# Expert stage rebuilt: weights split in 1024-column pieces, half of down taken whole, result rows without the residual

## The chip, the core and the metric

The kernel runs on one core of a Trainium2 chip. The metric is device time in microseconds for one launch. Before the change three runs took 1353.7, 1354.76 and 1357.26 us (median 1354.76). The profiled execution, from which every row below comes, took 1354.12 us, of which the profile's span holds 1352.3.

## The reference, cut to what matters

Two decoder layers over 1040 tokens (16 learned ones and 1024 of the input) of 1024 channels, float32. Layer 0 mixes by causal pooling, layer 1 by latent attention with 8 heads. Each layer ends with the same mixture of experts, and this is what the change is about:

```
p_g = softmax(x @ wr_g + br_g);  g = argmax(p_g)              # one of 4 groups
logit = x @ wr_e + br_e;  top 2 of the 8 experts of group g
gate = p_g[g] * softmax(the two logits)
for each of the two:  y = (silu(x @ w_gate[e]) * (x @ w_up[e])) @ w_down[e]
h = h + sum of gate * y over the two                          # 1024 -> 256 -> 1024 per expert
```

The output is the normed `h` of the last 1024 tokens. All 32 experts of a layer are evaluated: 32 x 3 MB of weights per layer are read from DRAM.

## The kernel before

The program has four stages: layer 0's mixer and router (to about 107 us), layer 0's experts (to about 437), latents, attention and layer 1's router (to about 977), layer 1's experts and the final norm.

**Products.** TensorE takes a float32 product in one of two ways. *Whole*: the float32 operands as they are. *In parts*: each operand is split into a rounded high part (a ScalarE copy to float32r, L1224) and a low remainder (a VectorE subtraction, L1225), and three products high x high, high x low, low x high are added up (`mm3`, L1229 to L1231).

**The expert loop** (`Moe.run`, L872) goes over e = 0 to 32 and works in one round on expert e's gate and up products and on expert e-1's down product. A gather (L776) brings up to 96 token rows of `h_d` from DRAM into a buffer `xg`. TensorE transposes them (`xpose`, L794), VectorE multiplies by the norm's gain (L796, two times 384 columns). Of the eight 128-row steps of gate and of up, four run whole (`whole`, L817) and four in parts (`halves`), on weights split in pieces of 512 columns (`piece`, four buffers). Silu and product give `hm` (L841, L842), two transposes and a split give `hT` (`turn`, L851), and `down` runs twelve passes of 512 columns into `py`, all in parts. `rows` (L870, VectorE) computes `py * gate + xg` in place in `xg`; a scatter (L782) writes the 96 rows to `y_d`, where each token has one row for its first expert and one for its second. The scatters of a layer are declared independent of each other, since their rows differ.

**The residual** is carried by the rows: the mixer and the attention's output are scaled (`PART`), so that `h_d` holds a quarter or a half of `h`, the gates are scaled alike, and the two rows of a token add up to the whole `h`. The next stage (`Mid.ask`, `add`) and the end (`final`) therefore read two tensors of 128 tokens each and add them.

**Order of the work.** Each engine runs its instructions in the order in which the program issues them. Around the experts that order is written by hand in `Moe.run`; in the other stages a planner (`Sched`) orders tasks by costs and due times that stand in the code. A ring of 17 slots of 1 MB holds the weights: SyncE issues the next load when a slot comes free. GpSimd issues gathers (four experts ahead, nine `xg` buffers) and scatters on one queue, in program order. Weights of the first 17 slots are loaded while the router still works.

The lines that the prediction speaks of, as they stand before:

```python
self.k.nc.vector.scalar_tensor_tensor(y[:CAP, c], py[:CAP], wt, y[:CAP, c], op0=OP.mult, op1=OP.add)   # rows, L870
for o in self.scat:
    k.tc.declare_no_dep(st.ins, o.ins, reason="rows of other slots")                                  # scatter in run
nc.sync.dma_start(out=self.h_d[t * 128:t * 128 + n, :], in_=k.h[t][:n])                               # store_tasks, L410
s.op("V", ready, 1130, lambda: add(h, h, c, op=OP.add), lambda end: then(i, c, end))                  # Mid.add2, L1660
c = [[m.fetch(t, j) for j in range(2)] for t in range(NT)]                                            # final
```

## Time and profile before

| | |
|---|---|
| median of three runs | 1354.76 us |
| profiled execution, its span | 1354.12 us, 1352.3 us |
| TensorE busy | 1257.1 us, 93% of the span |
| VectorE busy | 1063.2 us, 79% |
| ScalarE busy | 751.3 us, 56% |
| GpSimd busy | 306.7 us, 23% |
| DMA moved | 284.96 MB, mean 211 GB/s |

How to read it: PE is TensorE's matmul, PEld its weight loads (which overlap), DVE VectorE, ACT ScalarE, POOL GpSimd, SP SyncE; a q behind the name is the engine's sequencer, which issues DMAs. "L1224" is a line of the kernel. Ends of matmuls are modelled, so the distance from one start to the next says how long one takes, not the duration. In brackets stands how long the engine was idle before an instruction and what ended that. Times are in us, in groups also ns for the mean of one. A row by stretch gives its length, then the busy time and number of instructions of PE, PEld, DVE, ACT and POOL in this order, the granted clock, the DMA engines' busy share and GB/s. A row of a timeline gives start, duration, engine, line, operation, out<-in, shapes and number; a row of a DMA view gives number, size and the us from issue to landing. The granted clock (PEclk) is 1.00 at 2.4 GHz and 0.50 at 1.2 GHz.

### The profile page before, as it was taken

What the parts mean: (1) busy time and instruction counts of PE and PEld (TensorE: products, weight loads), DVE (VectorE), ACT (ScalarE), POOL (GpSimd) and SP (SyncE); (2) the same over time, 40 slices, a digit from 0 to 9 for tenths busy, and PEclk for the clock granted to TensorE, in tenths of its full rate; (3) what the DMA queues carried; (4) which work ended last, traced back from release to release, by engine and by line L of the source; (5) the groups of instructions that cost most, each with busy time, mean ns of one, the idle gap of its engine ahead of it and who ended that gap; (6) DMA issues with size and microseconds to landing.
All of it is one profiled execution on the core that took longest, in us unless ns stands there. A gap on an engine that the chain in (4) does not pass through costs nothing. (4 is left out here: it accounts for less than half of the span.)

```text
span 1352.3 us, 22774 instructions
## 1 busy us (share of the span) xinstructions
PE 1257.1 (93%) x8027; PEld 1091.9 (81%) x8027; DVE 1063.2 (79%) x2591; ACT 751.3 (56%) x1597; POOL 306.7 (23%) x443
## 2 busy tenths in 40 slices
PE   7988999999998899999999999999699999999950
PEld 5977888888886799898998998989588888888830
DVE  5777888888888886767778766678878888888857
ACT  3436655555565654656565556555466555556532
POOL 0113121121111352022231232221312112112013
PEclk8998999999999899999999999999699999999975
DMA  8936999999980800100000010048699999999236
GB/s 300 409 127 207 363 364 361 350 368 361 361 283 26 267 25 1 57 24 28 21 25 25 5 32 16 17 161 283 248 319 368 364 350 361 357 346 349 88 137 276
DMA packets 78763, 284.96 MB, mean 211 GB/s; under 512 B 20017, under 2 KB 27441, under 8 KB 62258
## 3 DMA queue, kind: packets, MB, share of 16 engines
q1 hardware_dynamic: 64306, 249.60, 50.8%
q0 software_dynamic: 14336, 33.84, 7.5%
q8 instruction: 65, 1.06, 0.3%
q14 instruction: 56, 0.46, 0.1%
HBM read 262.09 MB, written 37.81 MB: 222 GB/s over the span
## 5 line engine op out<-in xcount | busy, mean ns | idle before, releaser
L1229 PE MATMUL gu<-wp,xT 128*96 128x256 f32 x512 | 147.3, 288 | 0.0
L1231 PE MATMUL gu<-wp,xT 128*96 128x256 f32 x512 | 143.4, 280 | 0.0
L1230 PE MATMUL gu<-wp,xT 128*96 128x256 f32 x512 | 143.3, 280 | 0.0
L782 POOL DMA_INDIRECT y_d<-xg,di x46 | 45.5, 989 | 360.4 <-DVE xg L870 348.4
L1225 DVE TENSOR_TENSOR wp<-slotB,wp 128x512 fp32r<-128x512 f32 x160 | 106.9, 690 | 22.7 <-ACT wp L1224 21.8
L1229 PE MATMUL py<-wp,hT 128*96 128x512 f32 x256 | 113.1, 442 | 0.8 <-ACT hT L1224 0.8
L1224 ACT ACTIVATE wp<-slotB 128x512 fp32r<-128x512 f32 x160 | 96.0, 626 | 23.4 <-PE py L1231 19.7
L1231 PE MATMUL py<-wp,hT 128*96 128x512 f32 x256 | 101.8, 398 | 0.2
L1230 PE MATMUL py<-wp,hT 128*96 128x512 f32 x256 | 101.0, 394 | 0.0
L2121 POOL TENSOR_TENSOR hh<-hh,wt 128x512 f32<-128x512 f32 x56 | 72.4, 1292 | 111.3 <-ACT wt L2120 110.6
L1224 ACT ACTIVATE xT<-xq 128x384 fp32r<-128x384 f32 x64 | 33.6, 526 | 109.5 <-DVE xq L796 109.5
L1229 PEld LDWEIGHTS gu<-wp,xT 128*96 128x96 f32 x512 | 84.8, 166 | 0.1
L1231 PEld LDWEIGHTS gu<-wp,xT 128*96 128x96 f32 x512 | 83.2, 162 | 0.0
L1230 PEld LDWEIGHTS gu<-wp,xT 128*96 128x96 f32 x512 | 82.9, 162 | 0.1
L817 PE MATMUL gu<-slotB,xq 128*96 128x256 f32 x320 | 75.6, 379 | 0.0
L1957 ACT ACTIVATE P<-bank,sm 128x400 f32<-128x400 f32 (+3 forms) x112 | 59.5, 539 | 25.7 <-DVE sm L1947 25.5
L1710 DVE TENSOR_TENSOR T<-bank,T 128x512 fp32r<-128x512 f32 (+2 forms) x112 | 53.6, 495 | 20.8 <-ACT T L1706 19.9
L796 DVE TENSOR_TENSOR xq<-pt,ffg 128x384 f32<-128x384 f32 x128 | 64.9, 548 | 4.5 <-PE pt L794 4.5
L2124 DVE SCALAR_TENSOR_TENSOR hh<-bank,ri,hh 128x512 f32<-128x512 f32 x72 | 53.5, 746 | 17.0 <-PE bank L1231 16.6
L870 DVE SCALAR_TENSOR_TENSOR xg<-py,table,xg 96x512 f32<-96x512 f32 x92 | 64.4, 738 | 3.0 <-PE py L1231 2.9
L1225 DVE TENSOR_TENSOR wp<-hh,wp 128x512 fp32r<-128x512 f32 x82 | 54.8, 690 | 11.3 <-ACT wp L1224 10.9
L841 ACT ACTIVATE hm<-gu,table 96x256 f32<-96x256 f32 x64 | 30.0, 469 | 58.4 <-PE gu L1231 58.4
(375 smaller groups left out, 3891.7 us busy)
## 6 DMA issues: line engine op xcount, KB each, us to landing
slotB<-w_up SPq DMA_DIRECT2D x20, 1024.0 KB, 11.2
slotB<-w_down SPq DMA_DIRECT2D x20, 1024.0 KB, 13.7
slotB<-w_gate SPq DMA_DIRECT2D x20, 1024.0 KB, 14.6
hh<-w_gate SPq DMA_DIRECT2D x11, 1024.0 KB, 12.6
hh<-w_up SPq DMA_DIRECT2D x10, 1024.0 KB, 8.3
hh<-w_down SPq DMA_DIRECT2D x10, 1024.0 KB, 9.0
slotR<-w_gate SPq DMA_DIRECT2D x10, 1024.0 KB, 13.4
slotR<-w_up SPq DMA_DIRECT2D x10, 1024.0 KB, 10.7
```

The lines of the kernel that those rows point to most:

```text
L796: nc.vector.tensor_tensor(x[q], pt, self.r.g[:, 4 * q:4 * q + 4].unsqueeze(2).to_broadcast([128, 4, CAP]), op=OP.mult)
L817: nc.tensor.matmul(gu[:CAP, f * FE:f * FE + FE], lhsT=x[0][:, j], rhs=w[:, j], start=(f == 0 and j == 0), stop=False)
L870: self.k.nc.vector.scalar_tensor_tensor(y[:CAP, c], py[:CAP], wt, y[:CAP, c], op0=OP.mult, op1=OP.add)
L1224: nc.scalar.activation(dH, src, AF.Copy)
L1225: nc.vector.tensor_tensor(dL, src, dH.bitcast(F32), op=OP.subtract)
L1229: nc.tensor.matmul(out, lhsT=aH, rhs=bH, start=start, stop=False)
L1230: nc.tensor.matmul(out, lhsT=aH, rhs=bL, start=False, stop=False)
L1231: nc.tensor.matmul(out, lhsT=aL, rhs=bH, start=False, stop=stop)
L1710: nc.vector.tensor_tensor(dL, src, dH.bitcast(F32), op=OP.subtract)
L1957: nc.scalar.activation(self.P[hd, qp][a][:, x0:x0 + xe], tt[:, :xe], AF.Exp, bias=sm[:, 3:4], scale=SCALE, accum_out=sm[:, x:x + 1])
L2121: done(end), s.op("G", end + s.LAT, 1170, lambda: nc.gpsimd.tensor_tensor(k.h[i][:, cs], k.h[i][:, cs], x, op=OP.add), lambda end: s.relea ...
L2124: s.op("V", now + s.LAT, 70 + 1.04 * 512, lambda: nc.vector.scalar_tensor_tensor(k.h[i][:, cs], p, self.ri[hd, i], k.h[i][:, cs], op0=OP.m ...
```

## The change

- **Pieces.** Weights are split 1024 columns at a time (`piece(e, f, q)`: matrix f, half q), with three buffers instead of four. Gate and up run wholly in parts (48 passes of 256 columns). Of down's two 128-row steps the first runs whole, the second in parts.
- **Order in a round.** The first halves of expert e+1's gate and up (`G`, `U`) are split in round e, behind down; `G1`, `wd` and `U1` in their own round. x of expert e+1 is transposed, scaled (one instruction of 768 columns) and split early in round e. Expert 0 runs its first halves whole.
- **Rows.** `rows` is one ScalarE instruction of 1024 columns, `py * gate`, without the residual; `PART` is gone.
- **Layer 0's rows**: the next stage reads `h_d` and both rows and adds three tensors; two buffers are taken for each tile; the first two tiles of `h_d` are read at the end of the expert stage (`Mid.ahead`).
- **Layer 1's rows**: `h` is stored to `h_d` and to `y_d`, and each scatter adds its rows to `y_d` in DRAM. Entries without a token go to 96 rows behind the tokens'. The scatters are no longer declared independent. `final` reads one tensor.
- Six `xg` buffers, gathers three ahead. `final` takes the tiles in other groups; the constant `tri` is loaded with a later part.

```diff
-WHOLE = 4
-NX = 9
-GA = 4
+NX = 6
+GA = 3
...
+        self.sum = layer == 1
+        self.y_d = k.tc.dram_tile([S + CAP if self.sum else 2 * L, D], F32, name=f"y_d{layer}")
...
+    def targets(self, di, row, off):
+        V = self.k.nc.vector
+        if self.sum:
+            V.tensor_scalar(di, row, self.junk_row[:CAP], None, op0=OP.min)
+        else:
+            V.tensor_tensor(di, row, off, op=OP.add)
...
+            if self.sum:
+                late.append(t)
+                while late and (t not in self.tiles[-2:] or t == self.tiles[-1]):
+                    x = late.pop(0)
+                    nc.sync.dma_start(out=self.y_d[x * 128:x * 128 + 128, :], in_=k.h[x])
...
+        if self.r.sum:
+            return nc.gpsimd.indirect_dma_start(
+                out=self.r.y_d, out_offset=bass.IndirectOffsetOnAxis(ap=didx, axis=0),
+                in_=y[:CAP], in_offset=None, bounds_check=S + CAP - 1, oob_is_err=True, compute_op=OP.add)
...
+    def xpose(self, xg, fine=False):
+        pt = self.psum.tile([128, 2, 512], F32, name="pt", tag="pt", bufs=1)[:, :, :4 * CAP]
+        x = k.mws.tile([128, 8, CAP], F32, name="xq", tag="xq", bufs=1)
+                nc.tensor.transpose(pt[:, q, j * CAP:(j + 1) * CAP], xv[:CAP, 4 * q + j], k.ident[:CAP, :CAP])
+        n = 2 if fine else 1
+        w = 2 // n
+        for i in range(n):
+            a, b = i * w, (i + 1) * w
+            nc.vector.tensor_tensor(x[:, 4 * a:4 * b].rearrange("p (a b) c -> p a b c", a=w),
+                                    pt[:, a:b].rearrange("p a (b c) -> p a b c", b=4),
+                                    self.r.g[:, 4 * a:4 * b].rearrange("p (a b) -> p a b", a=w).unsqueeze(3).to_broadcast(
+                                        [128, w, 4, CAP]), op=OP.mult)
+    def part(self, x, a=0):
+        xs = [self.k.mws.tile([128, 8, CAP], F32R, name=f"xT{i}", tag=f"xT{i}", bufs=2) for i in range(2)]
+        split(self.k, xs[0][:, a:], xs[1][:, a:], x[:, a:])
+        return xs
+    def piece(self, e, f, q):
+        src = self.w(e, f)
+        src = src[:, q] if f == 2 else src[:, 4 * q:4 * q + 4]
+        t = [k.mw.tile([128, 1024], F32R, name=f"wp{i}", tag=f"wp{i}", bufs=PIECES) for i in range(2)]
+        if f < 2:
+            t = [x.rearrange("p (a b) -> p a b", a=4) for x in t]
+        split(k, *t, src)
+    def up(self, gu, xs, wp, f, q):
+        for j in range(4):
+            mm3(self.k.nc, gu[:CAP, f * FE:f * FE + FE], xs[0][:, 4 * q + j], xs[1][:, 4 * q + j], wp[0][:, j], wp[1][:, j],
+                q == 0 and f == 0 and j == 0, q == 1 and f == 1 and j == 3)
+    def whole(self, gu, x, e, f):
+        w = self.w(e, f)
+        for j in range(4):
+            self.k.nc.tensor.matmul(gu[:CAP, f * FE:f * FE + FE], lhsT=x[:, j], rhs=w[:, j], start=(f == 0 and j == 0), stop=False)
...
+    def turned(self, ph):
+        h0 = k.mws.tile([128, CAP], F32, name="hT", tag="hT", bufs=1)
+        hs = [k.mws.tile([128, CAP], F32R, name=f"hT{i}", tag=f"hT{i}", bufs=1) for i in range(2)]
+        nc.scalar.activation(h0, ph[:, 0], AF.Copy)
+        split(k, hs[0], hs[1], ph[:, 1])
+        return h0, hs
+    def down(self, e, h, wp):
+        nc, w = self.k.nc, self.w(e, 2)
+        py = self.psum.tile([128, 2, 512], F32, name="py", tag="py", bufs=1)
+        cs = [slice(q * 512, q * 512 + 512) for q in range(2)]
+            nc.tensor.matmul(py[:CAP, q], lhsT=h[0], rhs=w[:, 0, cs[q]], start=True, stop=False)
+        for q in range(2):
+            mm3(nc, py[:CAP, q], *h[1], wp[0][:, cs[q]], wp[1][:, cs[q]], False, True)
+        return py
+    def rows(self, py, wt, y):
+        self.k.nc.scalar.activation(y[:CAP], py[:CAP].rearrange("p a b -> p (a b)"), AF.Copy, scale=wt)
...
-            for o in self.scat:
+            for o in () if r.sum else self.scat:
                 k.tc.declare_no_dep(st.ins, o.ins, reason="rows of other slots")
             self.scat.append(st)
...
-        x = self.xpose(xgs[0])
-        wp = self.up_pieces(0)
-        x = self.part(x)
-        hm = None
+        x = self.xpose(xgs[0], fine=True)
+        xs, G, U, hm = None, None, None, None
         for e in range(NE + 1):
             prev, this = e > 0, e < NE
-            ga(e + GA)
-            if prev:
-                wd = self.down_pieces(e - 1, 0)
             if this:
                 gu = self.gu()
-                self.whole(x, e, gu, 0, range(WHOLE))
+                if prev:
+                    G1 = self.piece(e, 0, 1)
+                    self.up(gu, xs, G, 0, 0)
+                else:
+                    self.whole(gu, x, 0, 0)
+                    self.whole(gu, x, 0, 1)
+                    xs = self.part(x, 4)
+                    G1 = self.piece(0, 0, 1)
+            ga(e + GA)
+            if e + 1 < NE:
+                x = self.xpose(xgs[(e + 1) % NX])
             if prev:
-                hs = self.turn(hm)
-                wd += self.down_pieces(e - 1, 1)
+                wd = self.piece(e - 1, 2, 1)
+                if this:
+                    self.up(gu, xs, U, 1, 0)
+                ph = self.turn(hm)
+            if e + 1 < NE:
+                xs2 = self.part(x)
+            if prev:
+                hs = self.turned(ph)
             if this:
-                self.whole(x, e, gu, 1, range(WHOLE))
+                self.up(gu, xs, G1, 0, 1)
+                U1 = self.piece(e, 1, 1)
             if prev:
-                ps = self.down(hs, wd)
+                py = self.down(e - 1, hs, wd)
                 load(1)
-            if this and prev:
-                wp = self.up_pieces(e)
             if e + 1 < NE:
-                x2 = self.xpose(xgs[(e + 1) % NX])
+                G, U = self.piece(e + 1, 0, 0), self.piece(e + 1, 1, 0)
             if prev:
                 y = xgs[(e - 1) % NX]
-                self.rows(ps, r.table[:CAP, 0, e - 1:e], y)
+                self.rows(py, r.table[:CAP, 0, e - 1:e], y)
                 scatter(y, r.di[:CAP, e - 1:e])
             if this:
-                if e + 1 < NE:
-                    x2 = self.part(x2)
-                self.halves(x, gu, wp)
-                x = x2
+                self.up(gu, xs, U1, 1, 1)
+                xs = xs2
                 load(2)
                 hm = self.act(gu, r.table[:CAP, 1, e:e + 1])
...
+    def ahead(m):
+        m.k.hold(0)
+        for t in range(2):
+            m.fetch(t, None, m.k.h[t])
...
-    def ask(self, i, c):
+    def ask(self, i):
         k, t = self.k, self.ORDER[i]
-        if t == NT:
-            k.h[NT] = k.hp.tile([128, D], F32, name=f"h{NT}", tag=f"h{NT}", bufs=1)
-        elif t % 2 == 0:
-            k.hold(t // 2)
-        for j, x in enumerate((k.h[t], c)):
-            self.m.fetch(t, j, x)
-        self.got[i] = c
+        if i > 1:
+            if t == NT:
+                k.h[NT] = k.hp.tile([128, D], F32, name=f"h{NT}", tag=f"h{NT}", bufs=1)
+            elif t % 2 == 0:
+                k.hold(t // 2)
+            self.m.fetch(t, None, k.h[t])
+        self.got[i] = [self.free.pop(0) for j in range(2)]
+        for j in range(2):
+            self.m.fetch(t, j, self.got[i][j])
         self.nfetch = i + 1
...
-        s.op("V", ready, 1130, lambda: add(h, h, c, op=OP.add), lambda end: then(i, c, end))
+        s.chain(ready, *[("V", 1130, lambda x=x: add(h, h, x, op=OP.add)) for x in c], last="V", then=lambda end: then(i, c, end))
...
-        s.chain(ready, ("G", 2300, lambda: nc.gpsimd.tensor_tensor(h, h, c[:n], op=OP.add)), then=lambda end: self.added(i, c, end))
+        s.chain(ready, ("G", 2300, lambda: nc.gpsimd.tensor_tensor(h, h, c[0][:n], op=OP.add)),
+                ("V", 1130, lambda: nc.vector.tensor_tensor(h, h, c[1][:n], op=OP.add)), then=lambda end: self.added(i, c, end))
...
-    c = [[m.fetch(t, j) for j in range(2)] for t in range(NT)]
+    c = [k.work.tile([128, D], F32, name=f"c{t}") for t in range(NT)]
+    for t in range(NT):
+        m.fetch(t, 0, c[t])
...
-            c0, c1 = c[t]
-            s.chain(FINAL_START + 2920 * t + 1460, ("G", 2300, lambda c0=c0, c1=c1: nc.gpsimd.tensor_tensor(c0, c0, c1, op=OP.add)) if t in FINAL_POOL else
-                    ("V", 1130, lambda c0=c0, c1=c1: V.tensor_tensor(c0, c0, c1, op=OP.add)),
-                    ("A", 1040, lambda c0=c0, c1=c1, st=st, i=i: nc.scalar.activation(
-                        c1.bitcast(BF16)[:, :D], c0, AF.Square, accum_out=st[:, 0, i:i + 1])), then=squared)
+            def square(t=t, st=st, i=i):
+                junk = k.work.tile([128, D], BF16, name="fjunk", tag="fjunk", bufs=2)
+                nc.scalar.activation(junk, c[t], AF.Square, accum_out=st[:, 0, i:i + 1])
+            s.chain(FINAL_START + 1460 * t, ("A", 1040, square), then=squared)
...
```

## Rows read from the trace of the kernel before

**Rows 1.** Busy time by stretch, with clock, DMA share and GB/s

```profile
480.00:500.00 20.00, 20.00 (x133) 19.85 (x132) 16.01 (x54) 9.40 (x26) 10.79 (x19) 1.00 0.00 1
...
965.00:970.00 5.00, 1.19 (x16) 0.98 (x15) 4.79 (x23) 0.95 (x3) 1.26 (x3) 0.50 0.43 182
...
1200.00:1250.00 50.00, 50.00 (x310) 41.73 (x309) 43.90 (x75) 29.22 (x55) 10.08 (x10) 1.00 0.98 349
```

**Rows 2.** Timeline, one expert

```profile
200.46 1.89 PE L817 MATMUL gu<-slotB,xq 128*96 128x256 f32 x8
...
200.66 0.47 ACT L841 ACTIVATE hm<-gu,table 96x256 f32<-96x256 f32 x1 [0.84 <-PE gu L1231]
...
201.03 1.14 ACT L1224 ACTIVATE wp<-slotB 128x512 fp32r<-128x512 f32 x2
...
202.18 0.33 PE L851 MATMUL ph<-cb,hm 96*128 96x96 f32 x2
...
202.35 1.89 PE L817 MATMUL gu<-slotA,xq 128*96 128x256 f32 x8
...
204.53 0.39 PE L1231 MATMUL py<-wp,hT 128*96 128x512 f32 x1
...
204.96 1.33 ACT L1224 ACTIVATE wp<-slotB 128x512 fp32r<-128x512 f32 x2 [1.05 <-PE py L1231]
...
206.84 1.02 PE L794 MATMUL pt<-cb,xg 96*128 96x96 f32 x8
...
207.65 0.34 PE L1229 MATMUL gu<-wp,xT 128*96 128x256 f32 x1
...
210.53 1.89 PE L817 MATMUL gu<-slotA,xq 128*96 128x256 f32 x8
```

**Rows 3.** Groups by line and shape, 150 to 400 us; count | busy us, mean ns | idle

```profile
L1225 DVE TENSOR_TENSOR wp<-slotB,wp 128x512 fp32r<-128x512 f32 x106 | 71.0, 690 | 15.5 <-ACT wp L1224 14.8
L1224 ACT ACTIVATE wp<-slotB 128x512 fp32r<-128x512 f32 x106 | 63.7, 626 | 17.3 <-PE py L1231 14.7
...
L796 DVE TENSOR_TENSOR xq<-pt,ffg 128x384 f32<-128x384 f32 x48 | 24.3, 548 | 0.0
```

**Rows 4.** The same groups over the whole span

```profile
L2120 ACT ACTIVATE wt<-bank,ri 128x512 f32<-128x512 f32 x56 | 38.5, 688 | 41.7 <-PE bank L1231 34.6 <-POOL T L2039 2.9 <-DVE sm L1947 2.8
...
L1706 ACT ACTIVATE wo<-rawA 128x1024 fp32r<-128x1024 f32 x8 | 8.4, 1054 | 0.0
```

**Rows 5.** Timeline, the first expert

```profile
111.15 1.10 PE L794 MATMUL pt<-cb,xg 96*128 96x96 f32 x8 [0.48 <-DMA xg<-h_d,gi]
...
112.45 1.97 PE L817 MATMUL gu<-hh,xq 128*96 128x256 f32 x8 [0.20 <-DVE xq L796]
...
119.68 1.89 PE L817 MATMUL gu<-slotB,xq 128*96 128x256 f32 x8
```

**Rows 6.** Landing of the scatters (L782); loads and gathers at 1000 and at 1200 us

```profile
DMA to landing us min/median/max: 3.3/7.7/9.4
...
qr<-w_up SPq DMA_DIRECT2D x1, 1024.0 KB, 7.2
...
slotR<-w_up SPq DMA_DIRECT2D x2, 1024.0 KB, 19.3
...
xg<-h_d,gi POOLq DMA_INDIRECT x4, 10.7
```

**Rows 7.** Timeline of VectorE, the first addition after layer 0's experts

```profile
448.60 1.22 DVE L1660 TENSOR_TENSOR hh<-hh,qr 128x1024 f32<-128x1024 f32 x1
```

**Rows 8.** Timeline of the end

```profile
1308.92 12.91 SPq L1019 DMA_DIRECT2D cmb<-y_d  x16
1313.94 1.23 DVE L2323 TENSOR_TENSOR cmb<-cmb 128x1024 f32<-128x1024 f32 x1 [9.20 <-DMA cmb<-y_d]
...
1332.49 3.67 DVE L2310 SCALAR_TENSOR_TENSOR cmb<-cmb,fst,xg 128x1024 f32<-128x1024 f32 x3
...
1346.88 1.28 DVE L2310 SCALAR_TENSOR_TENSOR cmb<-cmb,fst,xg 128x1024 f32<-128x1024 f32 x1
```

More of the change, by code (lines that the diff above doesn't have):

```diff
@@ L353, in __init__ @@
         self.nx = c.tile([128, 1], I32, name=f"nx{layer}")
+        if self.sum:
+            self.junk_row = c.tile([128, 1], F32, name=f"junkrow{layer}")
         self.prior = []
@@ L544, in gates @@
         def gates(end):
-            part = 2 * PART[self.layer]
             def expo():
@@ L793, in xpose @@
             for j in range(4):
-                nc.tensor.transpose(pt[:, j, :], xv[:CAP, 4 * q + j], k.ident[:CAP, :CAP])
-            x.append(k.mws.tile([128, 4, CAP], F32, name=f"xq{q}", tag=f"xq{q}", bufs=1))
-            nc.vector.tensor_tensor(x[q], pt, self.r.g[:, 4 * q:4 * q + 4].unsqueeze(2).to_broadcast([128, 4, CAP]), op=OP.mult)
-        return x
-    def part(self, x):
-        k = self.k
-        xs = [k.mws.tile([128, 4, CAP], F32R, name=f"xT{i}", tag=f"xT{i}", bufs=2) for i in range(2)]
-        split(k, xs[0], xs[1], x[1])
-        return x[0], xs
@@ L805, in piece @@
-    def piece(self, src):
-        k = self.k
-        t = [k.mw.tile([128, 512], F32R, name=f"wp{i}", tag=f"wp{i}", bufs=PIECES) for i in range(2)]
-        n = src.shape[1] if len(src.shape) == 3 else 1
-        split(k, *([x.rearrange("p (a b) -> p a b", a=n) if n > 1 else x for x in t]), src)
-        return t
-    def whole(self, x, e, gu, f, js):
-        nc, w = self.k.nc, self.w(e, f)
-        for j in js:
-            nc.tensor.matmul(gu[:CAP, f * FE:f * FE + FE], lhsT=x[0][:, j], rhs=w[:, j],
-                             start=(f == 0 and j == 0), stop=False)
@@ L847, in turn @@
         k, nc = self.k, self.k.nc
-        hs = [k.mws.tile([128, 2, CAP], F32R, name=f"hT{i}", tag=f"hT{i}", bufs=2) for i in range(2)]
         ph = self.psum.tile([128, 2, CAP], F32, name="ph", tag="ph", bufs=1)
@@ L1004, in overflow, with fetch @@
             gu = self.gu()
-            for f in range(2):
-                self.whole(xs, NE - 1, gu, f, range(WHOLE))
-            self.halves(xs, gu, self.up_pieces(NE - 1))
+            for p in range(2):
+                for f in range(2):
+                    self.up(gu, xs, self.piece(NE - 1, f, p), f, p)
             hm = self.act(gu, wt[:CAP, 4:5])
-            ps = self.down(self.turn(hm), self.down_pieces(NE - 1, 0) + self.down_pieces(NE - 1, 1))
+            ps = self.down(NE - 1, self.turned(self.turn(hm)), self.piece(NE - 1, 2, 1))
             self.rows(ps, wt[:CAP, 3:4], k.xg[0])
             scatter(k.xg[0], di[:CAP, :1])
-    def fetch(self, t, j, c=None):
-        k, nc, r = self.k, self.k.nc, self.r
+    def fetch(self, t, j, c):
+        r = self.r
         n = NM if t == NT else 128
-        if c is None:
-            c = k.cmb.tile([128, D], F32, name="cmb", tag="cmb", bufs=k.ncmb)
-        nc.sync.dma_start(out=c[:n], in_=r.y_d[j * L + t * 128:j * L + t * 128 + n, :])
-        return c
+        a = (j or 0) * L + t * 128
+        self.k.nc.sync.dma_start(out=c[:n], in_=(r.h_d if j is None else r.y_d)[a:a + n, :])
 class Phase0:
@@ L1059, in load @@
         sc = self.sc.rearrange("p g d -> p (g d)")
[L1060 removed]
+        for t, c in ((sc, 0.0), (one, 0.0), (one[:1], 1.0)):
             nc.vector.memset(t, c)
@@ L2255, in experts @@
         k.mw = pool("mw", side=side)
-        k.xg = [(mwx if i < 3 else k.mwy).tile([128, D], F32, name=f"xg{i}") for i in range(NX - 3)]
+        k.xg = [mwx.tile([128, D], F32, name=f"xg{i}") for i in range(NX - 3)]
         k.xg.append(k.hp.tile([128, D], F32, name="xgh", tag=f"h{NT}", bufs=1))
@@ L2261, in experts @@
         m.run([loads[i] for i in todo] + loads[SLOTS:], len(loads) - SLOTS, last)
-        close(*[x for x in ("mps", "mw", "mwx", "mws", "mwy") if x not in stay])
-    experts(m0, loads + raw.loads(), p0.todo, "left", (), 3)
+        close(*[x for x in ("mps", "mw", "mwx", "mws") if x not in stay])
+    experts(m0, loads + raw.loads(), p0.todo, "left", (), 3, [lambda: Mid.ahead(m0)])
     close("ringB", "route0")
```

83 lines of the change are left out of this document (27 added, 56 removed).

## The prediction

> **What bounds the kernel now.** I read the table of busy time by stretch first, because a share over the whole span mixes four stages. In the two expert stages (about 111 to 437 us and 977 to 1304 us) TensorE is busy all of a stretch's 50 us at a granted clock of 1.00, its level of 2.4 GHz; VectorE has 43.9 of 50, ScalarE 29.2, and the DMA engines read 0.98 [rows 1]. The timeline of one expert then shows the same passes returning every 210.53 - 200.46 = 10.07 us with no wait in front of a TensorE group [rows 2]. So TensorE's own list sets the period, and 32 experts in each of two layers make it worth counting in hundredths. The transfers are nearly full too, but do not end last: a weight load lands 7.2 us after its issue early in the second expert stage and 19.3 us late in it [rows 6], so they fall behind slowly, against a ring of 17 slots.
>
> **An expert's period on TensorE.** Before [rows 2]: one matrix's four whole passes 202.18 - 200.46 = 1.72; two transposes 0.17; the other whole passes and twelve 512-column passes of down 206.84 - 202.35 = 4.49, so 2.77 for the twelve (0.23 each); eight transposes 0.81; twenty-four 256-column passes 210.53 - 207.65 = 2.88 (0.12 each). After: 48 of the 256-column passes, 5.76; down's whole half, two 512-column products with the columns of the four 256-column ones, 1.72; six three-pass ones 1.38; transposes 0.98. Sum 9.84 against 10.05 by the same counting: 0.2 us less.
>
> **Who must keep up.** VectorE loses the two residual additions, and ScalarE takes the scaling. The order on ScalarE is what I fear. With three pieces in the ring, U's cast for the next expert reuses the tile of down's piece, so it waits for down's last matmul; behind it on ScalarE queue the scaling of the rows, silu and the cast of the second gate piece; behind that cast, on VectorE, its low part and then the scaling of x; then x's cast and the copy of h for down's whole half. Durations: a 512-column cast is 0.626 and its low part 0.690 [rows 3]; a 1024-column cast 1.054 and scaling by a per-row factor out of PSUM 0.688 for 512 columns [rows 4], hence 0.688 + 512 x 0.83 ns = 1.12 for 1024; a 1024-column VectorE operation on two SBUF tensors 1.22 [rows 7]; 384 columns out of PSUM 0.548 [rows 3], so 0.95 for 768. Two casts take 1.14 together [rows 2], so an instruction starts 0.11 before the former ends; I take about that on VectorE too. ScalarE follows a 512-column pass 204.96 - 204.53 = 0.43 after its start [rows 2], which is 0.20 after TensorE goes on to its next. With TensorE's start on what comes behind down as 0: U's cast from 0.20, rows from 1.14, silu (0.47, [rows 2]) from 2.15, G1's cast 2.51 to 3.56, its low part 3.60 to 4.82, x's scaling 4.73 to 5.68, x's cast from 5.72 (0.85 by the cast's slope), h's copy 6.46 to 6.71, TensorE from 6.76. TensorE's own work up to there is 36 + 12 passes, 5.76, and transposes, 0.98: 6.74. A tie. Then 1.72 + 1.38 and a restart of about 0.1: 9.95. I take 9.95 us; the ends are 9.80 (TensorE dense) and 10.25 (the overlaps of 0.1 lost at three of the hops). For 30 experts that is 30 x -0.12 = -3.6 us a layer.
>
> **The first expert pays back.** Now it takes 119.68 - 111.15 = 8.53 [rows 5]. After, x of expert 1 is scaled and cast ahead of the last piece of expert 0: transposes and scaling 112.45 - 111.15 = 1.30 as now, whole passes 3.44 (to 4.7), transposes to 5.6, x's scaling to 6.7, x's cast to 7.55, U1's cast to 8.5, its low part to 9.75; twelve passes 1.44 to 11.2, and a hand-over. That is +2.8. Each layer: -3.6 + 2.8 = about -1. Buffers: nine rows become six and gathers run three ahead; a gather's lead falls to about two periods, 20 us, against a landing of 10.7 [rows 6], so nothing is priced.
>
> **The end.** It reads one tensor, not two. Before, from the first fetch at 1308.92 to the end of the span at 1352.3 is 43.4 [rows 8]. Eight fetches remain (4.2 MB), nothing is added. The first two transfers had landed at 1313.94, 5.0 after that fetch; today they are both halves of one tile, then they are two tiles. Two squares, 1.05 each as the 1024-column ScalarE operation [rows 4], and the reading of their sums end at 7.4 at most, a pair's eleven small operations of 0.2 end at 9.6. Before, the scalings ran from 1332.49 to 1348.16, 15.7 for eight scalings, one addition and five short chains; without the addition and with the same number of small operations, 14 to 15. Then 4.1 to the end as now: 28.2, so -15 (ends -11 and -19).
>
> **The middle.** Residual and two results are added instead of two halves: nine VectorE additions more, eight of 1.22 [rows 7], 9.8 in all, and 4.2 MB more read, two tiles of it ahead, behind the last weights. Where latents are projected TensorE has 20.00 of 20 us and VectorE 16.01 of them [rows 1]: there is room, but the first two tiles lie on the path (2 x 1.22). I take +4, ends 0 and 9.8. Where layer 1's router stores its rows, 8 x 0.52 MB more go out; at the 349 GB/s of the second expert stage 12 us of transfers. Before, the transfers were down to 0.43 of their time and 182 GB/s between 965 and 970 [rows 1], just before the layer's first gather, and the last two tiles' stores stand behind the last one that the gather needs; +2, ends 0 and 12. Halving factors, a shorter first constant, and a small gate operation: about 0, hidden under the loads of phase 0; 0.2 at most.
>
> **Sum**, against the profiled execution (1354.12, 0.6 below the median of 1354.76): -1 - 1 + 4 + 2 - 15 = -11, so **1343 us**.
>
> **A wait that is new.** In layer 1 scatters add in DRAM, and each waits on GpSimd for the one before to land. Behind it on that queue stand the gathers, and behind these TensorE. A plain scatter lands after 3.3 to 9.4 us, median 7.7 [rows 6], the low end where no weights load. The trace has no adding transfer: at least the 7.7 of now, at most twice the 9.4. It moves 96 rows, not the filled ones alone, and reads the target. I take 9.5, nearest to the loaded rows: under 9.95, at no cost. In the stage that cover is 0.45 us thin.
> The Trainium skill ("DMA: Bandwidth & Descriptors", Rules for kernel authors) says that an accumulating DMA's read and write are not held together, and to wait for the earlier one's semaphore; so these waits can't be overlapped away. The same page of the Trainium skill (Anatomy of one DMA) fits a transfer as 2.0 us + bytes / 436e3, an estimate of 2.9 us for 0.39 MB: by it the chain never binds; by the loaded row, at 7.7 for fewer rows, it nearly does. The row decides here, and no run yet shows the sum.
>
> **Rivals.**
> 1. *Scatters set layer 1's pace* (slower). One takes longer than the period; the gather's spare lead, about 8 us, is eaten, and then each of some 26 experts (those under loads) costs the excess. At 11.5 us: 26 x 1.55 - 8 = +32, 1375. From 10.9 on (26 x 0.95 - 8 = 17) the whole is slower than before. For it: landings up to 9.4 [rows 6], and DMA engines at 0.98, on top of which come the rows read to be added to. Against: 3.3 without loads, and a slower pace would itself thin the loads. Chance 0.20.
> 2. *ScalarE's circle is longer*: 10.25 a period, 60 x 0.30 = +18: 1361. For it: no slack in the walk. Against: ScalarE's wait ends 0.04 after the modelled end of the pass that it waits for (204.53 + 0.39 to 204.96, [rows 2]). Chance 0.13.
> 3. *TensorE stays dense*: 9.80, 60 x -0.15 = -9: 1334. For it: TensorE waits nowhere now. Chance 0.17.
> 4. *The stage is really held by transfers* and the change to the passes does nothing: 10.07 stays, 60 x 0.12 = +7: 1350. For it 0.98 [rows 1]; against, seventeen slots at three a period are 57 us of weights, and a load lands in 19.3 [rows 6]. Chance 0.05.
>
> **Numbers.** The forecast has 0.45: 1343, its own range 1334 to 1353. A measurement tells 0.3% (4 us) from no change: faster is under 1350.7. Faster: 0.40 of the forecast, all of rival 3, 0.03 of rival 4: 0.60. Slower: rival 1 (0.20) and two thirds of rival 2: 0.28. The rest, 0.12, is the same. The range: 1326 (rival 3 with the end at -19 and the middle at 0 to +4) to 1376 (rival 1).
>
> **What will show it.** Right: passes of one expert return every 9.9 to 10.0 us in layer 0, with a short wait in front of down's whole half, put down to ScalarE's hT; layer 1 the same; the last stretch near 28 us from first fetch. Wrong: GpSimd's scatter in layer 1 released by the DMA of y_d and not by ScalarE's rows, with waits of TensorE on gathered rows (rival 1); long waits before hT in both layers (rival 2); none (rival 3); TensorE waiting for weight slots (rival 4). In the middle, TensorE waiting for VectorE's additions beyond 4 us would refute that term.

## The result, and the profile after

| | before | changed |
|---|---|---|
| median, 19 runs of each | 1355.2 us | 1365.71 us |
| lowest to highest | 1352.98 to 1359.88 | 1356.18 to 1372.29 |
| profiled execution, its span | 1354.12, 1352.3 us | 1372.29, 1370.5 us |

The ratio is 1.0073, with a 95% interval of 1.0059 to 1.0087: slower, where 1343 us, faster, was the forecast. Times of the changed kernel lie further apart than those of the one before, and its profiled execution is its slowest; a second one is among the experiments.

**The walk through one expert came out to 0.03 us.** The timeline of the changed kernel in layer 0, against [rows 2]:

```profile
410.86 0.27 PE L1262 MATMUL gu<-wp,xT 128*96 128x256 f32 x1
...
411.06 1.06 ACT L1257 ACTIVATE wp<-slotB 128x1024 fp32r<-128x1024 f32 x1 [1.42 <-PE py L1264]
...
412.03 1.10 ACT L896 ACTIVATE hh<-py,table 96x1024 f32<-96x1024 f32 x1
...
413.03 0.45 ACT L863 ACTIVATE hm<-gu,table 96x256 f32<-96x256 f32 x1
...
413.38 2.00 ACT L1257 ACTIVATE wp<-slotB 128x1024 fp32r<-128x1024 f32 x2
...
414.46 1.23 DVE L1258 TENSOR_TENSOR wp<-slotB,wp 128x1024 fp32r<-128x1024 f32 x1 [0.47 <-ACT wp L1257]
...
415.60 0.95 DVE L821 TENSOR_TENSOR xq<-pt,ffg 128x768 f32<-128x768 f32 x1
...
416.58 0.85 ACT L1257 ACTIVATE xT<-xq 128x768 fp32r<-128x768 f32 x1 [1.21 <-DVE xq L821]
...
417.34 0.23 ACT L880 ACTIVATE hT<-ph 128x96 f32<-128x96 f32 x1
...
417.62 1.96 PE L889 MATMUL py<-slotB,hT 128*96 128x512 f32 x4
...
420.82 0.27 PE L1262 MATMUL gu<-wp,xT 128*96 128x256 f32 x1
```

With 410.86 as 0, the steps start at 0.20, 1.17, 2.17, 2.52, 3.60, 4.74, 5.72, 6.48 and 6.76; the forecast had 0.20, 1.14, 2.15, 2.51, 3.60, 4.73, 5.72, 6.46 and 6.76. The passes return after 420.82 - 410.86 = 9.96 us (9.95 forecast, 10.07 before). So the loop is what it was meant to be, and the time went elsewhere. Stretches of the changed kernel, against [rows 1]:

```profile
115.00:120.00 5.00, 2.63 (x22) 2.21 (x20) 3.26 (x4) 3.19 (x4) 0.40 (x1) 0.93 0.85 280
120.00:125.00 5.00, 5.00 (x24) 5.00 (x25) 3.55 (x4) 2.86 (x4) 0.00 (x0) 0.50 0.58 213
990.00:995.00 5.00, 0.00 (x0) 0.00 (x0) 0.00 (x0) 0.00 (x0) 0.00 (x0) 0.50 0.64 145
1200.00:1250.00 50.00, 49.17 (x337) 41.05 (x336) 40.53 (x45) 36.65 (x50) 15.46 (x10) 1.00 1.03 328
1250.00:1300.00 50.00, 45.95 (x303) 37.23 (x302) 35.14 (x39) 31.21 (x42) 15.14 (x10) 1.00 1.01 331
```

Three things are new. In the first expert of layer 0 the granted clock falls to 0.50, after TensorE had 2.63 busy us of the 5 before. At 990 us, where layer 1's experts should have begun, no engine does anything. And at 1200 to 1250 us TensorE is no longer full (49.17 of 50, and 45.95 in the next stretch), while the transfers move 328 GB/s at a busy share of 1.03 instead of 349 at 0.98.

The whole, cut at events that both timelines show (us; differences are taken before rounding):

| stretch | before | changed | difference |
|---|---|---|---|
| start to layer 0's first transposes | 111.2 | 109.5 | -1.7 |
| from there to layer 0's last down pass | 325.4 | 327.1 | +1.6 |
| to the first addition of the next stage | 12.0 | 14.9 | +2.8 |
| to layer 1's first gather | 523.9 | 534.3 | +10.4 |
| to layer 1's first transposes (the gather lands) | 4.2 | 9.6 | +5.4 |
| to layer 1's last down pass | 326.8 | 340.0 | +13.2 |
| to the first fetch of the end | 5.5 | 8.3 | +2.9 |
| to the end of the span | 43.4 | 26.9 | -16.5 |
| sum | 1352.3 | 1370.5 | +18.2 |

**Layer 1, where most is lost.** First the packets from 1020 to 1220 us by queue (number, MB, share of the 16 engines' time): weights are q1, rows are q0. The first fence is the kernel before, the second the changed one.

```profile
q1 hardware_dynamic: 10840, 60.88, 84.1%
q0 software_dynamic: 4480, 10.23, 14.7%
```

```profile
q1 hardware_dynamic: 9958, 55.98, 75.7%
q0 software_dynamic: 4211, 12.23, 26.5%
```

An expert's three matrices are 3 x 1.049 = 3.15 MB. Before, 60.88 MB in 200 us is one expert in 10.33 us; the passes take one in 10.09, which is why a load lands 7.2 us after its issue early and 19.3 late [rows 6]: the ring's lead was being eaten already. After, 55.98 MB is one in 11.24 us against passes that take 9.95. From the 24th expert on the lead is gone and the layer runs at the pace of its loads. From silu to silu six of its last eight experts take 11.71, 11.70, 11.21, 11.42, 11.17 and 11.32 us, and ScalarE's cast waits for a matrix:

```profile
1252.95 1.06 ACT L1257 ACTIVATE wp<-kT 128x1024 fp32r<-128x1024 f32 x1 [3.17 <-DMA kT<-w_up]
...
1264.65 1.06 ACT L1257 ACTIVATE wp<-hh 128x1024 fp32r<-128x1024 f32 x1 [3.16 <-DMA hh<-w_up]
```

Six periods before these are longer too, 10.15 to 10.46 us, and in four of them TensorE waits 0.3 to 0.4 us for gathered rows. The scatters of layer 1 (their waits for a landing, in us and number, and the time to landing):

```profile
  POOL y_d L798: 89.7, 13
...
DMA to landing us min/median/max: 5.3/9.6/10.5
```

They take 5.3 us to land where no weights load and 9.6 in the median of the 15 whose landing this trace holds (9.3 in that of all 32 in the second profile; 9.5 was the estimate, 7.8 has layer 0). For 89.7 us one scatter waited for the landing of another. The next scatter starts 0.79 us after a landing, so a link of the chain takes 10.4 us and not 9.6: from the third scatter to the 26th they start 10.44 us apart, more than the 9.95 of the passes, and come up to 8.3 us after the rows that they carry. By the prediction's own list this is the mark of rival 1.

### The profile page after: what moved, and what is told of

Same layout as the page of the kernel before. It is cut to its first block, busy times and chain, and to the rows that moved or that the text cites. A ratio compares the mean times of both kernels' runs of the same rounds, so it can differ in the third digit from the quotient of the medians.

```text
span 1370.5 us, 22966 instructions
## 1 busy us (share of the span) xinstructions
PE 1263.3 (92%) x8395; PEld 1095.5 (80%) x8395; DVE 1023.7 (75%) x2208; ACT 834.7 (61%) x1523; POOL 342.5 (25%) x437
## 3 DMA queue, kind: packets, MB, share of 16 engines
q0 software_dynamic: 14336, 38.03, 10.7%
## 5 line engine op out<-in xcount | busy, mean ns | idle before, releaser
L1262 PE MATMUL gu<-wp,xT 128*96 128x256 f32 x1008 | 291.4, 289 | 2.9 <-ACT wp L1257 2.9
L1263 PE MATMUL gu<-wp,xT 128*96 128x256 f32 x1008 | 285.2, 283 | 5.8 <-DVE wp L1258 5.8
L1264 PE MATMUL gu<-wp,xT 128*96 128x256 f32 x1008 | 284.3, 282 | 0.0
L1263 PEld LDWEIGHTS gu<-wp,xT 128*96 128x96 f32 x1008 | 164.4, 163 | 13.2 <-DVE wp L1258 8.6
L1262 PEld LDWEIGHTS gu<-wp,xT 128*96 128x96 f32 x1008 | 166.5, 165 | 7.9 <-ACT wp L1257 3.4
L1264 PEld LDWEIGHTS gu<-wp,xT 128*96 128x96 f32 x1008 | 164.9, 164 | 0.0
L1258 DVE TENSOR_TENSOR wp<-slotB,wp 128x1024 fp32r<-128x1024 f32 x99 | 119.5, 1222 | 29.5 <-ACT wp L1257 26.7
L1257 ACT ACTIVATE wp<-slotB 128x1024 fp32r<-128x1024 f32 x99 | 101.0, 1054 | 26.2 <-PE py L1264 26.0
L1262 PE MATMUL py<-wp,hT 128*96 128x512 f32 x128 | 76.1, 594 | 0.0
L1258 DVE TENSOR_TENSOR wp<-hh,wp 128x1024 fp32r<-128x1024 f32 x51 | 62.2, 1222 | 18.1 <-ACT wp L1257 17.2
L821 DVE TENSOR_TENSOR xq<-pt,ffg 128x768 f32<-128x768 f32 (+1 forms) x66 | 60.9, 926 | 17.6 <-PE pt L816 17.6
L1258 DVE TENSOR_TENSOR wp<-slotR,wp 128x1024 fp32r<-128x1024 f32 x48 | 58.2, 1223 | 15.6 <-ACT wp L1257 14.0
L1258 DVE TENSOR_TENSOR xT<-xq,xT 128x768 fp32r<-128x768 f32 (+1 forms) x64 | 60.0, 938 | 3.2 <-ACT xT L1257 3.2
L1985 DVE TENSOR_REDUCE mx<-bank 128x1 f32<-128x400 f32 (+3 forms) x112 | 55.4, 504 | 7.6 <-PE bank L1971 5.6
```

What stands on the lines that cost most here:

```text
L821: nc.vector.tensor_tensor(x[:, 4 * a:4 * b].rearrange("p (a b) c -> p a b c", a=w), pt[:, a:b].rearrange("p a (b c) -> p a b c", b=4), sel ...
L1257: nc.scalar.activation(dH, src, AF.Copy)
L1258: nc.vector.tensor_tensor(dL, src, dH.bitcast(F32), op=OP.subtract)
L1262: nc.tensor.matmul(out, lhsT=aH, rhs=bH, start=start, stop=False)
L1263: nc.tensor.matmul(out, lhsT=aH, rhs=bL, start=False, stop=False)
L1264: nc.tensor.matmul(out, lhsT=aL, rhs=bH, start=False, stop=stop)
```

## The experiments

Theory T: the adding scatters take time of the DMA engines from the weight loads. Rival O: each scatter's wait for the one before sets the pace. All times beside the kernel before on the same chip. First the changed kernel again.

> The changed kernel once more, for a second profile. In the first one layer 1's experts came every 9.94 us up to the sixteenth and every 11.2 to 11.7 us for the last five, the first adds to the latents 2.8 us later than before, layer 1's first gather was 13.2 us later and landed 5.4 us more late. Theory T (the adding scatters take time of the DMA engines from the weight loads, which come late at the end of layer 1) and rival O (each scatter's wait for the one before sets the pace) both expect the same again, within 4 us of 1366: 9.94 for about two thirds of the layer, then over 11.

1367.03 us, ratio 1.0071 [1.0046, 1.0096]; layer 1's stage 337.2 us, 56.75 MB of weights in the 200 us. The two profiles agree on all of the stretches above to within 3 us; layer 0's first silu, the end of the first expert's gate and up, came 15.4 us after the first transposes here, 13.1 in the first profile, 8.7 before the change.

### What the adding costs: e2, e3, e4

Each added line is the edit of the run named behind it; e4 also makes the second tensor.

```diff
-   bounds_check=S + CAP - 1, oob_is_err=True, compute_op=OP.add)
+   bounds_check=S + CAP - 1, oob_is_err=True)                       # e2: rows replace
+   bounds_check=S - 1, oob_is_err=False, compute_op=OP.add)         # e3: filled rows alone
-   out=self.r.y_d,
+   out=self.k.y2 if self.nsc % 2 else self.r.y_d,                   # e4: two tensors in turn
```

> Layer 1's scatters write their 96 rows instead of adding them (so the result lacks the residual and one of each token's two experts); the same rows, the same order, each still behind the one before. T: without the reading of the target the loads get back a part of their rate (295 instead of 265 to 280 GB/s of weights), no weight is late, 9.94 to the end, 7 to 9 us less than the changed kernel: about 1358. O: the chain of landings is as before, the last experts still take over 11 us, 1366.

> Layer 1's scatters add only the rows that hold a token (about two thirds of the 96); the others are dropped at the bounds check instead of going to spare rows. T: a third less of added traffic, the queue's share falls from 28% to about 20%, weights late for one or two experts at most: 5 to 8 us less than the changed kernel, 1359. O: a landing is 2 to 3 us shorter (6.5 to 7.5 instead of 9.6), so the chain no longer binds: also about 1358. Both agree here; it says what the spare rows cost.

> Layer 1's scatters add to two tensors in turn, so that each waits only for the last but one; the bytes stay the same (the second tensor's first contents are written during the latents, where transfers are idle; the result lacks what goes there). T: loads as slow as in the changed kernel, weights late at the end, last experts over 11 us: 1366, or some us worse since scatters bunch. O: no scatter waits, 9.94 to the end: 1357.

| | median us | ratio to before | layer 1's stage | weights, MB in 200 us |
|---|---|---|---|---|
| e2, no adding | 1355.92 | 0.9994 [0.998, 1.0007] | 329.1 | 61.79 |
| e3, filled rows alone | 1365.06 | 1.0062 [1.0043, 1.0081] | 336.2 | 56.86 |
| e4, two tensors | 1365.05 | 1.0081 [1.0055, 1.0106] | 335.5 | 55.26 |

The two queues of e2, as above:

```profile
q1 hardware_dynamic: 11037, 61.79, 82.6%
q0 software_dynamic: 4480, 13.02, 17.9%
```

e2 keeps the order of the scatters and all 96 rows and takes away the adding: behind the first expert no period of the layer is over 9.96 us. Its scatters land in 8.0 us, so that the chain fits too; e2 alone does not tell T from O. e4 keeps the adding and takes away the order: the waits of layer 1's scatters (us in all, times, longest) end with ScalarE in all but one of 32 cases, and casts still wait for weights.

```profile
POOL y_d_y L799 <- ACT xg L897: 69.3, 10, 7.8
...
POOL y_d L799 <- ACT hh L897: 37.7, 5, 8.8
...
POOL y_d_y L799 <- DMA y_d<-hh,di: 6.8, 1, 6.8
...
ACT wp L1258 <- DMA slot<-w_up: 3.9, 1, 3.9
ACT wp L1258 <- DMA slotR<-w_up: 3.8, 1, 3.8
```

With no scatter waiting, the loads alone hold the stage at 335.5 us: T stands, and O is not needed for it. But O is not idle. In e1 the two longest waits of TensorE for gathered rows, which stand behind the scatters in GpSimd's queue, make periods of 13.19 and 10.81 us, 4.1 of the 8.1 us by which that layer's periods exceed 9.95 in all; behind the longer one the granted clock is 0.66 in the mean from 1215 to 1220 us.

```profile
1215.00 1.35 PE L816 MATMUL pt<-cb,hh 96*128 96x96 f32 x8 [1.72 <-DMA hh<-h_d,gi]
```

e3 was a miss for T as I had it: a fifth less time of q0 (21.2% against 26.5%) gave the loads almost nothing. That needed a sharper form.

### Where the rows lie: e5, e13, e14

```diff
-   put("iota128", np.broadcast_to(t, (128, 128)))
+   put("iota128", np.broadcast_to(np.where(t < CAP, t % 6 * 16 + t // 6, t), (128, 128)))
```

The constant is compared with a token's rank to give its slot; e5 has this and e3's edit, e13 this alone, e14 this in the kernel before.

> Layer 1 adds only filled rows, and in both layers the filled slots of an expert are spread over all 96 partitions (the r-th token goes to partition r mod 16 * 6 + r / 16) instead of the first two thirds. Theory T in a sharper form, H (the DMA engines that carry the rows are the bound, each carries the rows of six neighbouring partitions, and a weight load ends with its slowest engine, which is why dropping the spare rows alone gave 56.9 MB of weights in 200 us against 56.0 to 56.8): with four or five rows on each engine the loads get 60 to 62 MB in 200 us, as with plain scatters, no weight is late, layer 1's stage 329 instead of 336 to 340, total 1357. Rival A (the adding itself costs, wherever the rows lie): as without spreading, 57 MB, stage 336, 1365.

> The changed kernel with the slots spread over the partitions, but layer 1 still adds all 96 rows, spare ones too. H (the fullest engine sets how fast weights come): the gathers put four or five rows on an engine instead of six, the adding still six on each, so about half of the gain of both edits together: 58 to 59 MB of weights in 200 us (56.0 to 56.8 without, 60.1 with both), layer 1's stage 331 to 334, 1360. Rival G (all of the gain comes from the gathers): 60 MB, stage 328, 1355. Rival K (all of it comes from the adding): 56.5 MB, 336 to 340, 1366.

> The kernel before with its slots spread over the partitions in the same way; nothing else. H: weight loads no longer fall behind in layer 1: at 1200 to 1240 us they land 8 to 12 us after their issue instead of 19 to 23. The time stays within 2 us of before, since no weight was late there. If the even spread does nothing without the adding: 19 us as before.

| | median us | ratio to before | layer 1's stage | weights, MB in 200 us |
|---|---|---|---|---|
| e5, spread, filled rows alone | 1352.75 | 0.9984 [0.997, 0.9998] | 327.6 | 60.06 |
| e13, spread, all 96 added | 1361.08 | 1.0059 [1.0042, 1.0076] | 333.7 | 57.94 |
| e14, before, spread | 1351.28 | 0.9978 [0.9965, 0.9991] | 325.3 | 62.81 |

e5 against e3 differs by nothing but the partition in which a row lies, and q0 has about the same share (21.9 and 21.2%); yet the loads gain 3.2 MB and no weight is late. First e3, then e5:

```profile
q1 hardware_dynamic: 10141, 56.86, 77.7%
q0 software_dynamic: 4384, 10.25, 21.2%
```

```profile
q1 hardware_dynamic: 10677, 60.06, 80.0%
q0 software_dynamic: 4472, 10.57, 21.9%
```

e13 lies between, as H says, but not clearly: the changed kernel has 1.0073 [1.0059, 1.0087], and e10 below, without spreading, 57.2 MB and 333.1 us. What e13 does show is the price of the chain alone. No cast waits for weights, its scatters start 10.43 us apart (third to 26th; 10.04 in e5), TensorE waits seven times for gathered rows, 3.9 us in all, and its stage is 6.1 us longer than that of e5, which has neither wait. So O has a price of its own where T is taken away. First two scatters in turn, then the waits from 1015 to 1330 us (us in all, times, longest):

```profile
1134.58 1.44 POOL L798 DMA_INDIRECT y_d<-hh,di  x1 [7.37 <-DMA y_d<-hh,di]
...
1145.26 1.44 POOL L798 DMA_INDIRECT y_d<-xg,di  x1 [7.45 <-DMA y_d<-hh,di]
```

```profile
PE pt L816 <- DMA xg<-h_d,gi: 2.0, 3, 0.9
...
PE pt L816 <- DMA hh<-h_d,gi: 1.9, 4, 0.8
```

In the kernel before, the loads stop falling behind: they land 7.5 us after their issue late in layer 1, where [rows 6] has 19.3. Its time falls by 3.1 us, a little more than the 2 expected.

```profile
slotR<-w_up SPq DMA_DIRECT2D x2, 1024.0 KB, 7.5
...
xg<-h_d,gi POOLq DMA_INDIRECT x4, 7.1
```

Scatters that meet few other transfers show the same. The last three of layer 0, where the queues are nearly idle, land after 3.5 to 3.7 us in the eleven profiles without spreading and after 3.0 to 3.1 in the five with it. In layer 1 the fastest takes 5.2 us in e1 and in e3 alike, though e3 drops about a third of the rows, and 4.4 in e11 and e12, which drop and spread. Fewer rows alone gain nothing; evenly spread ones do.

The trace does not number the engines. That each carries the rows of six neighbouring partitions is inferred, and these runs would look alike if something else that belongs to a partition were the narrow place. The Trainium skill ("DMA: Bandwidth & Descriptors", Why a DMA increments its semaphore by 16 and not by 1) lets a transfer of 96 partitions run on 16 engines, which agrees with six rows on each. The same page of the Trainium skill (Anatomy of one DMA) fits a transfer as 2.0 us + bytes / 436e3, an estimate of 2.9 us for 0.39 MB, which does not agree: in the changed kernel's two profiles no adding scatter landed under 5.2 us.

### The first expert: e6

```diff
     G1 = self.piece(0, 0, 1)
+    U1 = self.piece(0, 1, 1)
...
-    U1 = self.piece(e, 1, 1)
+    if prev:
+        U1 = self.piece(e, 1, 1)
```

> Expert 0's second piece of up is split before x of expert 1 is scaled and cast, instead of behind it; nothing else. In the changed kernel the first silu comes 12.1 to 15.4 us (layer 0) and 15.5 us (layer 1) after the first transposes, before the change 8.7; TensorE waits 1.5 and 0.9 us for that piece and its granted clock then falls to 0.50. Theory C (the wait is the order of the pieces, and the clock it costs follows from the wait): first silu after 8.7 to 9.2 us in layer 0 at a clock of 1.00, after 11 to 12 in layer 1, which starts at 0.50: 3.5 to 6 us less there and 3.5 here, 1358. Rival: the clock falls anyway, from the wait for the first gather: 1.5 to 2.4 us less in each layer only, 1362.

1356.15 us, ratio 0.9996 [0.9984, 1.0008]. The first silu comes after 10.0 us in layer 0 and 13.3 in layer 1: less than hoped, since one wait of 0.90 us stays, but the clock holds where it had fallen. First the two waits of the changed kernel, then the same stretch in e6:

```profile
118.66 0.36 PE L1262 MATMUL gu<-wp,xT 128*96 128x256 f32 x1 [1.46 <-ACT wp L1257]
...
119.92 0.53 PE L1263 MATMUL gu<-wp,xT 128*96 128x256 f32 x1 [0.90 <-DVE wp L1258]
```

```profile
120.00:125.00 5.00, 4.36 (x38) 4.36 (x39) 5.00 (x6) 4.32 (x7) 1.28 (x1) 1.00 0.71 248
```

Behind these waits the changed kernel's passes start 0.21 us apart instead of 0.12 in these 5 us. Theory C holds for layer 0 in what the order of the pieces costs. That the fall of the clock follows from the two waits is not shown: e11 below keeps the changed order and has both waits, its clock stays at 1.00, and its first silu comes after 12.0 us.

```profile
119.14 0.36 PE L1262 MATMUL gu<-wp,xT 128*96 128x256 f32 x1 [1.46 <-ACT wp L1257]
...
120.40 0.36 PE L1263 MATMUL gu<-wp,xT 128*96 128x256 f32 x1 [0.90 <-DVE wp L1258]
```

```profile
120.00:125.00 5.00, 4.60 (x40) 4.60 (x41) 4.58 (x6) 4.01 (x6) 0.39 (x1) 1.00 0.63 223
```

In the other eleven profiles with both waits it fell. The whole gain of e6, about 10 us, is more than the 3 to 5 and 2 us of the two first experts; the rest was not separated. The stretch to layer 1's first gather, which the edit does not touch, is 529.8 us here and 534.3 in the first profile.

### Between the layers: e7, e8, e9, e10, e11

```diff
-   room = [k.xg[1], 0]
+   room = [k.xg[3], 0]                              # e7, e10
+   k.xg[1], k.xg[3] = k.xg[3], k.xg[1]              # e10
-   nc.sync.dma_start(out=self.y_d[...], in_=k.h[x])  # e8: during the latents instead
-   for j in range(2):
+   for j in range(1):                               # e9, and one addition less
-   AHEAD = (0, 5)
+   AHEAD = (0, 1)                                   # e11, on top of e5
```

> The overflow code, which follows each expert stage, takes its small tiles from row buffer 3 instead of 1. With six buffers expert 31's rows lie in buffer 1 (31 mod 6), and the trace of the changed kernel shows the first memset there waiting 7.5 and 9.6 us for the last scatter's landing; with nine buffers it was buffer 4. Theory B (this collision makes the latents begin 2.8 us later): first addition 12.0 us after the last down pass instead of 14.9, and about 0.5 us at the end of layer 1, where the fetch waits for the landing anyway: 3 us less, 1363. Rival: the additions wait for the landing in any case: no change, 1366.

> As with the overflow code's tiles moved to row buffer 3, and in addition expert 31's rows lie in a buffer whose memory nothing takes directly after the experts (list entries 1 and 3 change places). With the first edit alone ScalarE's first cast of the next stage still waited 4.1 us for that scatter's landing, since its tile takes the buffer's memory. Theory B': both waits gone, the first addition 12.0 us after the last down pass as before the change (14.2 to 14.9 so far), 3 us less than the changed kernel in this stage: 1361 to 1363. Rival: the first fetch of y_d waits for the landing in any case and the additions come no earlier than 14: 1366.

> The changed kernel, but the stage after layer 0's experts adds only the residual and the first expert's row of each token; the second row is neither read nor added (so the result lacks it). Two tiles are in flight as before this edit. Theory D (the third tensor costs its 8 x 1.22 us of VectorE additions and the reading where TensorE waits for the first tiles): from the first addition to layer 1's first gather 525 to 527 us instead of 529 to 534, 6 us less in all, 1360. Rival F (the two tiles in flight and the clock that falls to 0.50 while TensorE waits for the second scatter landing and the first tiles are what costs, not the bytes and the additions): 529 to 532, 1364.

> Layer 1's sums are begun during the latents (h as it is before the attention is stored to y_d there, when transfers idle; the result lacks the attention's part of the residual) instead of at layer 1's router, where 4.2 MB then compete with the first weights. Theory S (these stores delay the first gather): from the first addition to the first gather 532 us instead of 534, the gather lands 4.2 us after its issue instead of 9.0 to 9.6, so 6 us less: 1360. Rival: the late landing is due to the weight loads or to the gather's own queue: no change, 1366.

> The version with spread slots and without spare rows, and of the five weight loads that the router issues with its last tile only one is issued there, the other four behind layer 1's first gathers. Theory S' (the gather lands 9 us after its issue because more than 12 MB of weights and stores are queued before it; without the stores of y_d it landed in 4.0): 4 to 5 us after its issue instead of 8.7, and with spread slots the later loads are still in time: 4 us less than 1352.8, so 1349. Rival: the loads that start later make weights late at the end of layer 1: 1353 or more.

| | median us | ratio to before | last down pass to first addition | to first gather | gather lands |
|---|---|---|---|---|---|
| e7 | 1362.45 | 1.0054 [1.0036, 1.0073] | 14.1 | 531.3 | 8.8 |
| e10 | 1360.16 | 1.0052 [1.0035, 1.0068] | 12.1 | 535.1 | 8.9 |
| e9 | 1358.83 | 1.0039 [1.0024, 1.0053] | 14.9 | 526.3 | 9.9 |
| e8 | 1357.88 | 1.0026 [1.0012, 1.0039] | 14.9 | 530.7 | 4.0 |
| e11 | 1345.7 | 0.9948 [0.992, 0.9975] | 14.4 | 529.1 | 3.6 |

*The collision* is there. Rows of expert 31 lie in buffer 31 mod 6 = 1, where the overflow code, and after it the memory of ScalarE's next tile, waits for their landing; before it was buffer 31 mod 9 = 4. First the changed kernel's wait, then what was left of it in e7:

```profile
442.13 0.06 DVE L991 MEMSET xg<- 128x1 f32 x1 [7.51 <-DMA y_d<-xg,di]
```

```profile
440.81 3.73 ACT L1317 ACTIVATE wH<-slotA,gk 128x320 fp32r<-128x320 f32 x8 [4.06 <-DMA y_d<-xg,di]
```

e7 moved the first wait and not the second, a miss; e10 moved both, and the addition comes 12.1 us after the last pass as before the change. What it gives in the end was not settled: the next stretch lasts 529 to 535 us in kernels that do not touch it, more than the 2.8 us. *The third tensor*: without it 526.3 us, of 523.9 before, so it costs 3 to 9 us by the same spread; D fits better than F, by one profile. *The gather's landing*: rows of the changed kernel, of e8 and of e11, each the first gather of layer 1 and the transposes that wait for it:

```profile
985.67 1.02 POOL L791 DMA_INDIRECT xg<-h_d,gi  x1 [3.71 <-ACT xg L909]
...
995.24 1.52 PE L816 MATMUL pt<-cb,xg 96*128 96x96 f32 x8 [6.32 <-DMA xg<-h_d,gi]
```

```profile
980.53 1.02 POOL L791 DMA_INDIRECT xg<-h_d,gi  x1 [3.72 <-ACT xg L909]
...
984.57 1.10 PE L816 MATMUL pt<-cb,xg 96*128 96x96 f32 x8 [0.78 <-DMA xg<-h_d,gi]
```

```profile
978.01 1.02 POOL L791 DMA_INDIRECT xg<-h_d,gi  x1 [3.72 <-ACT xg L909]
...
981.65 1.10 PE L816 MATMUL pt<-cb,xg 96*128 96x96 f32 x8 [0.38 <-DMA xg<-h_d,gi]
```

Either 4.2 MB less in front of it, of stores (e8) or of weights that are not needed yet (e11), and it lands in 4 us. In e11 the loads that start later are still in time.

### All together: e12

> All mending edits together: only filled rows added, slots spread over the partitions, expert 0's second piece of up before x of expert 1, expert 31's rows and the overflow tiles out of the way, four loads behind the first gathers. By the single effects (spread -13 from 1366, first expert -7, buffers -3, loads -4): 1339. If the effects share waits (the first gather's landing and the first expert's clock are neighbours), 1345.

1336.99 us, ratio 0.9888 [0.9867, 0.9909]: 1.1% faster than the kernel before, and better than the sum of single effects (1339). It is the changed kernel with e5's, e6's, e10's and e11's edits. Its stretches: first silu after 10.0 and 11.7 us, 12.1 to the first addition, 528.4, a landing of 3.5, 324.7 for layer 1's stage (every period but the first and the last 9.94 to 9.96), 7.3 and 26.0 for the end.

## Why the prediction was wrong

- **The step that failed is "under 9.95, at no cost"**, the price of layer 1's adding scatters. It failed twice. The landing was estimated well (9.5, measured 9.3 to 9.6), but a link of the chain is the landing and the 0.79 us until the next scatter starts: 10.4, over the period. And the sum had no term for what the adding takes from the weight loads: 3.15 MB in 11.24 us instead of 10.33. Either is enough to cost: e4, without the chain, loses to late weights (335.5 us for the stage), and e13, with weights in time, to the chain (333.7). Together they cost 8 to 11 us (337.2 and 340.0 against 329.1 of e2, which has neither).
- **Rival 1 had the sign, the place and half of the mechanism.** Its mark, a scatter released by the landing of y_d, is in the trace with 89.7 us, and so are TensorE's waits on gathered rows, 0.3 to 0.4 us and in e1 up to 1.72. By its own sum a link of 10.44 costs 26 x 0.49 - 8 = 5 us; e13, where nothing else is late, has 4.5 in its periods. What it left out are the weights. **Rival 4** was put at 0.05 with "seventeen slots at three a period are 57 us of weights, and a load lands in 19.3". The same rows say that the landing grew by 12 us in 200. That is a rate; it has to be held against the lead over the whole layer, and any further load on the queues raises it.
- **The period and the gain of 0.12 us were right**, in layer 1 as long as rows and weights came in time, with the tie in front of down's whole half; rivals 2 and 3 fall. Measured over layer 0, 10.09 became 9.95.
- **"The first expert pays back", +2.8**: the order of the pieces was right, the size was not. First silu +4.4 us and the next period +1.9, 6.3 in all. In e11, with the same two waits (1.46 and 0.90 us) and the clock at 1.00, it is +3.3 and +0.4; the rest is the clock of 0.50 behind the waits, which had no price. In layer 1, where the first expert starts at 0.50 (the row of 990 to 995 us), the first silu comes 15.5 us after the transposes instead of 8.7 and the next period is 11.6 instead of 10.1: 8.3 us, in e2 as well, and more than half of what that stage lost.
- **The middle, +4 and +2**: measured +18.6. The third tensor cost 3 to 9, inside its ends of 0 and 9.8. The stores of y_d were priced where they are issued, +2; they cost where the gather queues behind them and the weights, +5.4, inside the ends too. The collision of buffer 1, +2.8, was not seen: "nine rows become six" was checked against the gathers' lead alone, not for what the last expert's buffer is used for next.
- **The end, -15**: from the first fetch it was -16.5 (26.9 us, forecast 28.2); the first fetch, behind the last adding scatter, comes 2.9 us later, so -13.6.
- In the sum, -1 became +1.6 in layer 0 and +13.2 in layer 1 (first expert +8.3, periods at 9.95 -4.1, what they took beyond that +10.9, the last expert and its down product -2), +6 became +18.6, and -15 became -13.6; with 1.7 us less at the start, which was priced at nothing, +18.2 in an execution that lies 6.6 above the median.

## What to carry to other kernels

Where transfers are full, ask of a changed transfer how much time it takes from the others, and compare rates: a landing that grows over a stage says that a lead is being spent. A link of a chain is its landing and the time until the next one starts. When two limits lie close together, taking one away gains almost nothing (e4), and that does not clear it. Rows moved by index need not be spread evenly; here their places alone decided how fast the weights came (e14). And after a change in the number of buffers, look at what the last one in use is wanted for next.

## What was not expected of the hardware

- A scatter that adds takes more of the engines' time than its bytes say: q0 had 17.9% for 13.02 MB with e2's, 26.0 to 26.5% for 12.03 to 12.23 MB with the adding, and the loads 61.79 against 55.98 to 56.75 MB in the same 200 us.
- Moving filled rows to other partitions, with nothing else changed, took a weight load's landing from 19.3 to 7.5 us and a gather's from 10.7 to 7.1.
- Waits of 1.46 and 0.90 us of TensorE, close together, were followed by a granted clock of 0.50 in eleven profiles of twelve; in e11 they were not. The 0.90 alone was not in either of two (e6, e12).
